# Where the two halves of an attention output are added: on VectorE and GpSimd, or by an accumulating load

## The chip, the cores and the metric

The kernel runs on one core of a Trainium2 chip. Its time is the device time of one execution in microseconds; the figure to predict is the median of several executions. Names of the engines as the profile writes them: PE is TensorE's matrix multiplication, PEld its loading of weights, DVE is VectorE, ACT is ScalarE, POOL is GpSimd, and SP is SyncE, which here does nothing but issue transfers (DMAs). ACT and POOL can issue transfers too.

## The reference

One step of a hybrid encoder with two layers, of width 1024, on 1024 prompt tokens and on 8 streams of 16 sample tokens. Layer A has sliding-window attention with its own K and V, layer B has chunked attention over K and V that are shared; each is followed by a squared-ReLU MLP with 4096 hidden units.

```python
def attend(q, k, v, bias, sink):
    s = jnp.einsum('bqhgd,bkhd->bhgqk', qg, k) * (HEAD_DIM ** -0.5)   # 16 heads, 4 KV heads, d = 64
    s = s + bias                                   # A: ALiBi, 2 chunks back; B: relative bias, 8 chunks back
    p = softmax(s)                                 # A: with a learned sink per head
    o = jnp.einsum('bhgqk,bkhd->bqhgd', p, v)
    return o.reshape(b, tq, N_HEADS * HEAD_DIM)

for layer in range(2):
    hp = hp + attend(...) @ w_o[layer]
    hp = hp + square(relu(rmsnorm(hp, g_mlp[layer]) @ w_up[layer])) @ w_down[layer]
```

## The kernel before

Tokens are in nine tiles of 128: tiles 0 to 7 are the prompt, tile 8 (`ST`) the sample. All matrix products are of float32 numbers that are split into a high part, rounded to `float32r`, and the low rest. `split` does this with a copy on ScalarE (or GpSimd) and a subtraction on VectorE. A product then takes three matmuls: high by high, high by low, low by high.

Each layer runs through four stages: attention, the output projection (`wo_phase`), the MLP's first product (`mlp_up`) and its second (`mlp_down`). The change is in the first two.

**Attention.** The prompt's work is cut into 32 groups `(t, j)`, a query tile and a KV head with its four query heads, in two passes: heads 0 and 1 for all tiles, then heads 2 and 3. For a group, `score_a` or `score_b` makes the scores on PE, the row minimum on DVE, the exponential on ACT and the normalisation of the probabilities `p` on POOL (lines L403 in A, L481 and L526 in B). Scores run two or three steps ahead of their use. `V(g)` then transposes `p` on PE (L324), splits it, and multiplies it with V (`pv_mm`, L331 and L332). V's high and low parts lie side by side in the columns of one operand, so the result `ps_pv` has 128 rows: rows 0 to 63 are the product with the high part of V and rows 64 to 127 that with the low part. **The two halves must be added**, and that is where the change is. Between a group's matmuls the kernel weaves those of other work, among it the projections of the next tiles and, late in the stage, the output projections `WO(t, half)`.

In layer A (`o2=0`), `pv_out` copies the lower half from PSUM on ACT (L357) and adds the halves on DVE with two additions (L359) into a tile `oT`; after the second group of a tile one store sends it to DRAM (`oTd`, L1540). In layer B (`o2=1`), `pv_store` copies all 128 rows on ACT (L346) and stores both halves apart in `oTd` with four transfers of 64 KB from SP (L351).

**Output projection.** `WO` inside the attention stage and `load_o` in `wo_phase` fetch the attention's output of a tile by `load_halves`, split it and multiply it with the output weights. In A that is one load of 256 KB (L337). In B a second load brings the other half (L339), and an addition joins them: on POOL inside the attention stage, and on DVE in `wo_phase` (both L341). In B the high part of the split inside the attention stage is made on POOL too (L130).

The order of instructions on every engine is fixed when the program is built: a scheduler places them by an estimate of when each can start. At run time an engine takes its instructions in that order, and one that waits holds up all behind it. On SP and POOL this holds for transfers as well: an issue waits until what it needs is there.

Of the kernel before, what the change touches and what calls it, by code (L numbers as in the profile page):

```python
# [8 lines left out]
F32 = mybir.dt.float32  # L9
F32R = mybir.dt.float32r  # L10
AF = mybir.ActivationFunctionType
ALU = mybir.AluOpType
# [4 lines left out]
P = 128  # L17
D = 1024
KC = D // P
NT = 8  # L20
# [74 lines left out]
class Build:  # L95
# [238 lines left out]
    def load_halves(self, layer, half, t, a, b, e=None):  # L334
        nc = self.nc
        src = self.oTd[layer][half][t]
        nc.sync.dma_start(a, src[:, 0])  # L337
        if self.o2[layer] and t < NT:
            nc.sync.dma_start(b(), src[:, 1])  # L339
            e = e or (nc.gpsimd if self.o2[layer] == 1 else nc.vector)  # L340
            e.tensor_tensor(a, a, self.last, ALU.add)  # L341
# [10 lines left out]

    def pv_out(self, apool, pv, oT, j):
        nc = self.nc
        t = apool.tile([64, 2, 2, P], F32, tag="pvt", name="pvt", bufs=1)
        pv4 = pv.rearrange("p (a b q) -> p a b q", a=2, b=2)
        nc.scalar.copy(t, pv4[64:128])  # L357
        for par in range(2):
            nc.vector.tensor_tensor(  # L359
                oT[par * 64 : par * 64 + 64, 2 * (j % 2) : 2 * (j % 2) + 2, :],  # L360
                pv4[0:64, :, par, :],
                t[:, :, par, :],
                ALU.add,
            )
# [278 lines left out]
    def wo_phase(self, layer, sx, x8, wo):  # L643
        nc = self.nc
        with ExitStack() as st:
            self.psum_pools(st, f"wo{layer}", dict(m=(4, 1), g=(3, 1)), dict(m="m", n="g"))
            work = self.pool(st, f"wow{layer}")
# [18 lines left out]
            def load_o(t, z):  # L666
# [3 lines left out]
                self.last = oh.bitcast(F32)  # L670
                self.load_halves(layer, 1, t, o, lambda: self.last, nc.vector)
# [586 lines left out]
    def run(self):  # L1258
# [9 lines left out]
        with ExitStack() as top:  # L1268
# [21 lines left out]
            def dram(shape, name):  # L1290
                return dp.tile(shape, F32, tag=name, name=name)
# [3 lines left out]
                    [dram([P, 2 if t < NT and CFG[l]["o2"] else 1, 4, P], f"oTd{l}_{b}_{t}")  # L1295
# [10 lines left out]
            self.o2 = [c["o2"] for c in CFG]  # L1306
# [57 lines left out]
    def attention(self, layer):  # L1364
# [18 lines left out]
        with ExitStack() as st:  # L1383
# [25 lines left out]
            hts, qTs, qss, kss, probs, oTs, xr = {}, {}, {}, {}, {}, {}, {}  # L1409
# [121 lines left out]
            def O(g, pv):  # L1531
                t, j = groups[g]
                if self.o2[layer]:
                    self.pv_store(apool, pv, self.oTd[layer][j // 2][t], j)
                    return
                if j % 2 == 0:
                    oTs[t] = work.tile([P, 4, P], F32, tag="oT", name="oT")
                self.pv_out(apool, pv, oTs[t], j)
                if j % 2 == 1:
                    nc.sync.dma_start(self.oTd[layer][j // 2][t][:, 0], oTs[t])  # L1540
# [35 lines left out]
            def addend():  # L1576
                self.last = self.scratch([P, 4, P], F32, "o2")
                return self.last

            def WO(t, half):  # L1580
                o = self.scratch([P, 4, P], F32, "o")
                self.load_halves(layer, half, t, o, addend)
# [243 lines left out]
def make_plan(tail, second):  # L1826
    plan = {}
    for s in range(2 * NT):
# [29 lines left out]
        la=3, prio=0, xt={('A', 8): 'x', ('B', 7): 'x', ('B', 0): 'keep', ('B', 4): 'keep'}, late=0, eng='cgu', k2=3, q2=9, lead=3, sf=0, up=(99, 2, 0, 3), ld=((9, 9, 10, 10), (11, 11, 12, 13), (26, 27, 28, 29)), n='g', q='g', qrb=1, np=3, bias_bufs=3, p_bufs=3, psp=(), wr='mmmm', wt=(0, 0, 2, 0, 2, 2, 0, 0, 2), rx=1, kd=1, o2=0, sb=0),  # L1858
    dict(banks=dict(g=(4, 1), s=(3, 1), m=(1, 1)), q_bufs=4, order={}, second=SECOND[1], plan=make_plan({15: [('A', 0)], 17: [('A', 1)], 19: [('A', 2)], 21: [('A', 3)], 23: [('A', 4)], 25: [('A', 5)], 27: [('A', 8)], 28: [('A', 7)], 29: [('A', 6)], 31: [('B', 0), ('B', 4), ('B', 1)], 32: [('B', 5), ('B', 2), ('B', 3)]}, SECOND[1]),
        la=2, prio=1000, xt={('B', 0): 'keep', ('B', 4): 'keep', ('B', 1): 'hh', ('B', 5): 'hl', ('B', 2): 'hh', ('B', 3): 'hl'}, late=0, eng='Ogu', k2=3, q2=6, lead=9, sf=0, up=(4, 2, 0, 99), ld=((11, 11, 11, 11), (11, 11, 11, 11), (26, 27, 28, 29)), n='g', q='g', qrb=2, np=2, bias_bufs=2, p_bufs=10, psp=(), wr='mmmm', wt=(0, 0, 0, 1, 1, 1, 1, 1, 2), rx=0, kd=1, o2=1, sb=3),  # L1860
# [45 lines left out]
```

## Time and profile before

| | |
|---|---|
| median of 3 runs | 2360.16 us (2359.15 to 2361.63) |
| the profiled execution's own time | 2354.01 us |
| its span, first to last instruction | 2352.2 us |
| mean granted clock of TensorE | 0.997 |
| PE busy | 2271.4 us, 97% of the span |
| DVE busy | 1715.4 us, 73% |
| ACT busy | 1332.4 us, 57% |
| POOL busy | 635.3 us, 27% |
| DMA | 392.70 MB, mean 167 GB/s |

Attention A runs from the start to about 380 us, the projections behind it to about 445, and the MLP of layer A to about 1140. Attention B lasts to about 1620, its last projections to about 1663, and the MLP of layer B to the end. In rows of groups, the count stands behind `x`, then come the busy time in us, the mean of one in ns, and the idle time of the engine just before, with what ended it. The issue of a transfer by SP is not counted as busy time of any engine.

### The profile page before, as it was taken

Reading aid. Unit: us, or ns where it says so; the run is one execution under the profiler, and the core shown is the slowest. Engines: PE = TensorE matmul, PEld = TensorE weight load, DVE = VectorE, ACT = ScalarE, POOL = GpSimd, SP = SyncE. Lnnn points to the kernel's source line nnn. Section 1 sums busy time; section 2 is a strip of 40 time slices with the busy share of each in tenths; the row PEclk is TensorE's granted clock in tenths of the full one; section 3 lists DMA queues with packets and bytes.
Section 4 is the critical chain, followed back from the end, with each engine's and each line's share of the span. In section 5 each row is a group of like instructions: output and inputs, shape, how many; then the busy total and the mean of one; then the engine's idle time right before and its main releaser. Section 6 shows DMA issues by size and latency. Waiting matters only on the chain.

```text
span 2352.2 us, 33396 instructions
## 1 busy us (share of the span) xinstructions
PE 2271.4 (97%) x11429; PEld 1893.3 (80%) x11429; DVE 1715.4 (73%) x3075; ACT 1332.4 (57%) x2684; POOL 635.3 (27%) x950
## 2 busy tenths in 40 slices
PE   7998999899999999999999999998899999999999
PEld 6787887788888888777877788887788888888787
DVE  6788786766656578899577877777666566678987
ACT  3777674655555555344377666665655555565443
POOL 4334332313213111002333434344132132110011
PEclk9999999999999999999999999999999999999999
DMA  7335546234434677748653655555244343977567
GB/s 253 127 113 163 171 147 202 95 122 160 137 111 151 218 230 177 267 147 214 183 157 113 193 157 177 174 168 184 69 156 138 113 162 107 284 209 199 175 169 192
DMA packets 226715, 392.70 MB, mean 167 GB/s; under 512 B 51592, under 2 KB 126288, under 8 KB 226448
## 3 DMA queue, kind: packets, MB, share of 16 engines
q1 hardware_dynamic: 188816, 283.58, 37.4%
q0 software_dynamic: 36432, 102.26, 15.9%
q10 hardware_dynamic: 1296, 4.72, 0.5%
q8 instruction: 90, 1.47, 0.2%
q14 instruction: 81, 0.66, 0.1%
HBM read 236.51 MB, written 156.85 MB: 167 GB/s over the span
## 4 chain that ended last, share of the span: by engine, by line
PE 74%; DVE 9%; DMA 9%; ACT 3%; issue 3%; POOL 1%; SPq 0%; ACTq 0%; DVEq 0%; POOLq 0%
PE ps_c L743 6%; PE ps_c L744 6%; PE ps_c L745 6%; PE ps_x L743 5%; PE ps_x L745 5%; PE ps_x L744 5%; PE ps_mm L217 3%; PE ps_mm L219 3%; PE ps_mm L218 3%; PE ps_y L745 2%; PE ps_y L743 2%; PE ps_y L744 2%; PE ps_tr L324 2%; DMA a<-hd 2%; DVE w L134 1%
## 5 line engine op out<-in xcount | busy, mean ns | idle before, releaser
L744 PE MATMUL ps_c<-w,a 128*128 128x512 f32 x960 | 374.7, 390 | 6.9 <-DVE w L134 6.9
L743 PE MATMUL ps_c<-w,a 128*128 128x512 f32 x960 | 375.1, 391 | 5.1 <-DVE x L1174 3.1
L745 PE MATMUL ps_c<-w,a 128*128 128x512 f32 x960 | 374.3, 390 | 0.0
L908 POOL DMA_DIRECT2D hd<-h x272 | 148.9, 550 | 594.8 <-ACT h L817 378.2
L743 PEld LDWEIGHTS ps_c<-w,a 128*128 128x128 f32 x960 | 180.6, 188 | 46.3 <-issue 4.7
L744 PEld LDWEIGHTS ps_c<-w,a 128*128 128x128 f32 x960 | 180.7, 188 | 46.1 <-DVE w L134 9.0
L745 PEld LDWEIGHTS ps_c<-w,a 128*128 128x128 f32 x960 | 180.5, 188 | 37.5
L128 ACT CAST a<-a 128x1536 fp32r<-128x1536 f32 x80 | 118.6, 1482 | 149.5 <-DMA a<-hd 149.5
L217 PE MATMUL ps_mm<-w,hh 128*128 128x512 f32 x432 | 172.7, 401 | 8.8 <-POOL w L185 3.3
L134 DVE TENSOR_TENSOR a<-a 128x1536 fp32r<-128x1536 f32 x80 | 140.5, 1756 | 45.7 <-ACT a L128 45.7
L219 PE MATMUL ps_mm<-w,hl 128*128 128x512 f32 x432 | 171.7, 398 | 1.5 <-DMA hl<-hTd 1.4
L218 PE MATMUL ps_mm<-w,hh 128*128 128x512 f32 x432 | 170.8, 396 | 1.3 <-DVE w L190 1.1
L743 PE MATMUL ps_x<-sx,w 128*128 128x512 f32 (+1 forms) x408 | 157.8, 387 | 3.7 <-ACT h L864 2.7
L128 ACT CAST w<-s 128x2048 fp32r<-128x2048 f32 x56 | 107.1, 1912 | 92.2 <-DVE s L1060 80.7
L128 ACT CAST w<-ru 128x512 fp32r<-128x512 f32 (+1 forms) x160 | 110.0, 708 | 83.9 <-PE ps_y L744 32.0
L745 PE MATMUL ps_x<-sx,w 128*128 128x512 f32 (+1 forms) x408 | 154.1, 378 | 0.0
L744 PE MATMUL ps_x<-sx,w 128*128 128x512 f32 (+1 forms) x408 | 154.1, 378 | 0.0
L134 DVE TENSOR_TENSOR w<-s,w 128x2048 fp32r<-128x2048 f32 x56 | 128.1, 2288 | 32.4 <-ACT w L128 32.3
L1179 POOL DMA_DIRECT2D xp<-o x28 | 36.3, 1296 | 411.8 <-ACT o L1162 390.2
L134 DVE TENSOR_TENSOR ptl<-ps_tr,pth 128x512 fp32r<-128x512 f32 x180 | 122.4, 685 | 24.1 <-ACT pth L128 18.2
L134 DVE TENSOR_TENSOR w<-ru,w 128x512 fp32r<-128x512 f32 (+1 forms) x160 | 126.6, 793 | 14.7 <-ACT w L128 14.6
L816 ACT ACTIVATE h<-h 128x512 f32<-128x512 f32 (+1 forms) x102 | 61.9, 607 | 122.6 <-DVE h L866 93.5
(274 smaller groups left out, 6131.4 us busy)
## 6 DMA issues: line engine op xcount, KB each, us to landing
a<-hd SPq DMA_DIRECT2D x80, 768.0 KB, 6.2
hd<-h POOLq DMA_DIRECT2D x272, 192.0 KB, 2.5
ru<-in_w_up SPq DMA_DIRECT2D x64, 512.0 KB, 3.9
r<-in_w_down SPq DMA_DIRECT2D x32, 1024.0 KB, 10.0
xp<-o POOLq DMA_DIRECT2D x28, 768.0 KB, 9.4
o<-oTd SPq DMA_DIRECT2D x50, 256.0 KB, 5.0
x<-xp SPq DMA_DIRECT2D x23, 512.0 KB, 5.2
xp<-xo SPq DMA_DIRECT2D x18, 512.0 KB, 2.8
```

Of the source, the lines that this page charges most:

```text
L128: a = nc.scalar.copy(hi, src)
L134: return a, e.tensor_tensor(lo, src, hi.bitcast(F32), ALU.subtract)
L217: nc.tensor.matmul(ps, a, w[:, 0, k, :], start=(k == 0), stop=False)
L218: nc.tensor.matmul(ps, a, w[:, 1, k, :], start=False, stop=False)
L219: self.lp = nc.tensor.matmul(ps, b, w[:, 0, k, :], start=False, stop=(k == KC - 1))
L324: self.lp = nc.tensor.transpose(pt[:, i, :], get(i), self.ident)
L743: a = mm(ps, ah, bh, start=first, stop=False, skip_group_check=True)
L744: mm(ps, ah, bl, start=False, stop=False, skip_group_check=True)
L745: return a, mm(ps, al, bh, start=False, stop=last, skip_group_check=True)
L816: a = nc.scalar.activation(t, src, AF.Relu)
L908: return lambda p, z: self.nc.gpsimd.dma_start(self.hd[c // 4][:, p, c % 4], z)
L1179: nc.gpsimd.dma_start(dst, z, accum_op=ALU.add)
```

## The change

Both layers now store the two halves apart with `pv_store`. `load_halves` loads the first half on SP as before, and then issues from POOL a second transfer that adds the other half to it on its way (`accum_op`), once the first has landed. `pv_out`, the tile `oT`, the second load's tile and the additions on DVE and POOL are gone.

```diff
-    def load_halves(self, layer, half, t, a, b, e=None):
+    def load_halves(self, layer, half, t, a):
         nc = self.nc
         src = self.oTd[layer][half][t]
         nc.sync.dma_start(a, src[:, 0])
-        if self.o2[layer] and t < NT:
-            nc.sync.dma_start(b(), src[:, 1])
-            e = e or (nc.gpsimd if self.o2[layer] == 1 else nc.vector)
-            e.tensor_tensor(a, a, self.last, ALU.add)
+        if t < NT:
+            nc.gpsimd.dma_start(a, src[:, 1], accum_op=ALU.add)
...
-    def pv_out(self, apool, pv, oT, j):
-        nc = self.nc
-        t = apool.tile([64, 2, 2, P], F32, tag="pvt", name="pvt", bufs=1)
-        pv4 = pv.rearrange("p (a b q) -> p a b q", a=2, b=2)
-        nc.scalar.copy(t, pv4[64:128])
-        for par in range(2):
-            nc.vector.tensor_tensor(
-                oT[par * 64 : par * 64 + 64, 2 * (j % 2) : 2 * (j % 2) + 2, :],
-                pv4[0:64, :, par, :],
-                t[:, :, par, :],
-                ALU.add,
-            )
...
-                self.last = oh.bitcast(F32)
-                self.load_halves(layer, 1, t, o, lambda: self.last, nc.vector)
+                self.load_halves(layer, 1, t, o)
                 self.split(oh, ol, o)
...
             def O(g, pv):
                 t, j = groups[g]
-                if self.o2[layer]:
-                    self.pv_store(apool, pv, self.oTd[layer][j // 2][t], j)
-                    return
-                if j % 2 == 0:
-                    oTs[t] = work.tile([P, 4, P], F32, tag="oT", name="oT")
-                self.pv_out(apool, pv, oTs[t], j)
-                if j % 2 == 1:
-                    nc.sync.dma_start(self.oTd[layer][j // 2][t][:, 0], oTs[t])
+                self.pv_store(apool, pv, self.oTd[layer][j // 2][t], j)
...
             def WO(t, half):
                 o = self.scratch([P, 4, P], F32, "o")
-                self.load_halves(layer, half, t, o, addend)
+                self.load_halves(layer, half, t, o)
```

By the built programs, PE has the same instructions in both, in an order that differs in places of the two attention stages and of `wo_phase`. DVE loses 64 additions in A and 2 in B, POOL loses 14 additions in B and gains 32 accumulating loads, 16 in each layer. SP gains 128 stores in A and loses 16 there, and loses 16 loads in B. Three places show how the order moves; lines below the changed functions have lower numbers in the changed kernel (L403 becomes L388, L481 becomes L466, L1540 is gone).

On SP in attention A, around the store of tile 1's first output (`oTd_0_1`; KT is the transposed K, whose halves are copied across by two transfers, `qu` and `kb` belong to the sample's units), the rows before:

```order
L545 DMA qu<-qT8d_0_125 128x128
L546 DMA qu<-qT8d_0_125 64x128
L547 DMA qu<-qT8d_0_125 64x128
L549 DMA kb<-kT8d_133 128x32
L313 DMA KT<-KT 64x4x128
L314 DMA KT<-KT 64x4x128
L1540 DMA oTd_0_1_76<-oT 128x512
L1421 DMA x<-in_x_prompt 128x1024
```

and the same place in the changed program:

```order
L349 DMA oTd_0_1_76<-pvt 64x2x128 x4
L530 DMA qu<-qT8d_0_125 128x128
L531 DMA qu<-qT8d_0_125 64x128
L532 DMA qu<-qT8d_0_125 64x128
L534 DMA kb<-kT8d_133 128x32
L313 DMA KT<-KT 64x4x128
L349 DMA oTd_0_1_76<-pvt 64x2x128
L314 DMA KT<-KT 64x4x128
L349 DMA oTd_0_1_76<-pvt 64x2x128 x3
L1404 DMA x<-in_x_prompt 128x1024
```

Eight small stores take the place of one large one, four of them ahead of the unit's loads and one between the two copies of KT.

On POOL in attention A, around the first output projection (`qrs` is a norm of the queries, `kc` and `uks` belong to the sample's units, `p` is the normalisation), the rows before:

```order
L238 TENSOR_TENSOR qrs<-qms,mhalf 128x8
L403 TENSOR_SCALAR p<-p,li 128x256 x4
L568 COPY uks<-kc 128x2x64
L403 TENSOR_SCALAR p<-p,li 128x256 x4
L569 TENSOR_TENSOR uks<-kc,uks 128x2x64
L558 TENSOR_TENSOR kc<-kc,gq 128x128
```

and in the changed program:

```order
L238 TENSOR_TENSOR qrs<-qms,mhalf 128x8
L339 DMA o<-oTd_0_0_75 128x512
L388 TENSOR_SCALAR p<-p,li 128x256 x4
L553 COPY uks<-kc 128x2x64
L554 TENSOR_TENSOR uks<-kc,uks 128x2x64
L388 TENSOR_SCALAR p<-p,li 128x256 x4
```

The accumulating load of tile 0 now stands ahead of a group's normalisations of `p`.

On POOL near the end of attention B (`xp` is the store of a projected tile, `mrs` a norm), the rows before:

```order
L1616 DMA xp_112<-xo 128x1024
L341 TENSOR_TENSOR o<-o,o_16937 128x512
L130 COPY oh<-o 128x512
L481 TENSOR_SCALAR p<-p,li 128x640 x2
L568 COPY uks<-kc 128x2x64
L341 TENSOR_TENSOR o<-o,o_16948 128x512
L569 TENSOR_TENSOR uks<-kc,uks 128x2x64
L130 COPY oh<-o 128x512
```

and in the changed program:

```order
L1588 DMA xp_112<-xo 128x1024
L339 DMA o<-oTd_1_5_107 128x512
L339 DMA o<-oTd_1_2_104 128x512
L130 COPY oh<-o 128x512
L466 TENSOR_SCALAR p<-p,li 128x640 x2
L553 COPY uks<-kc 128x2x64
L554 TENSOR_TENSOR uks<-kc,uks 128x2x64
L339 DMA o<-oTd_1_3_105 128x512
L130 COPY oh<-o 128x512
```

The additions are replaced by accumulating loads, and the cast `oh` stands right behind the issue whose landing it needs.

More of the change, by code (lines that the diff above doesn't have):

```diff
@@ L1294, in run @@
                 [
-                    [dram([P, 2 if t < NT and CFG[l]["o2"] else 1, 4, P], f"oTd{l}_{b}_{t}")
+                    [dram([P, 2 if t < NT else 1, 4, P], f"oTd{l}_{b}_{t}")
                      for t in range(NTILE)]
@@ L1305, in run @@
             self.qT8d = [[dram([P, 512], f"qT8d{l}_{j}") for j in range(KV)] for l in range(2)]
-            self.o2 = [c["o2"] for c in CFG]
             self.kT8d = [dram([P, KV, P], f"kT8d{l}") for l in range(2)]
@@ L1408, in attention @@
             second = cfg["second"]
-            hts, qTs, qss, kss, probs, oTs, xr = {}, {}, {}, {}, {}, {}, {}
+            hts, qTs, qss, kss, probs, xr = {}, {}, {}, {}, {}, {}
             x_src = self.x_in if A else lambda t: self.xd[t]
@@ L1574, in U @@
                 return self.unit(up, small, layer, bp, j, v8, gq8, ck, cv)
-            def addend():
-                self.last = self.scratch([P, 4, P], F32, "o2")
-                return self.last
             def WO(t, half):
                 o = self.scratch([P, 4, P], F32, "o")
-                self.load_halves(layer, half, t, o, addend)
+                self.load_halves(layer, half, t, o)
                 kind = cfg["wt"][t] if half else 0
```

4 lines of the change are left out of this document (2 added, 2 removed).

## The prediction

> **What bounds the kernel now.** I read the page first: busy shares and the shares of the chain that ended last.
>
> ```profile
> PE 2271.4 (97%) x11429; PEld 1893.3 (80%) x11429; DVE 1715.4 (73%) x3075; ACT 1332.4 (57%) x2684; POOL 635.3 (27%) x950
> PE 74%; DVE 9%; DMA 9%; ACT 3%; issue 3%; POOL 1%; SPq 0%; ACTq 0%; DVEq 0%; POOLq 0%
> ```
>
> TensorE (PE) is busy for 97% of the span, and the change takes no matmul away. So only time in which PE stands idle can be won, and only new idle time can be lost. The next view cuts the four stretches that the change touches: attention A, the projection phase behind it, attention B with its projections, and the end of B.
>
> ```profile
> core 0: us, PE busy (x) PEld busy (x) DVE busy (x) ACT busy (x) POOL busy (x), PEclk, DMA share, GB/s
> 60.00:380.00 320.00, 304.94 (x1677) 251.74 (x1676) 257.88 (x832) 230.34 (x670) 118.27 (x214) 0.99 0.49 152
> 380.00:450.00 70.00, 63.71 (x359) 52.70 (x358) 52.13 (x77) 34.99 (x64) 28.52 (x26) 1.00 0.40 136
> 1140.00:1590.00 450.00, 432.30 (x2363) 359.09 (x2362) 338.47 (x941) 291.54 (x806) 188.13 (x257) 1.00 0.54 167
> 1590.00:1670.00 80.00, 67.03 (x387) 55.07 (x386) 60.66 (x96) 44.07 (x91) 32.48 (x29) 0.96 0.43 145
> ```
>
> PE idles 320 - 304.94 = 15.1 us in attention A, 6.3 behind it, 17.7 in attention B and 13.0 at its end. That is 52 us in all, and the first 15 are where most of the removed work stood. What ended them is in the list of PE's waits between 60 and 380 us (waited for, total, times, longest):
>
> ```profile
> PE ps_mm L176 <- DVE xo L1614: 2.3, 3, 1.5
> PE ps_s L380 <- ACT p L395: 2.2, 4, 0.9
> PE ps_pv L331 <- ACT pth L128: 2.1, 1, 2.1
> PE ps_tr L324 <- POOL p L403: 1.7, 2, 0.9
> PE ps_s L380 <- DMA KT<-KT: 1.2, 2, 0.9
> ```
>
> No wait is large and no engine owns them. PE follows a fixed order with short slack to all the others.
>
> **The change part by part.** First, VectorE (DVE) in attention A. The rows of the removed additions and of the output copies, before and as layer B already does them:
>
> ```profile
> L359 DVE TENSOR_TENSOR oT<-ps_pv,pvt 64x256 f32<-64x256 f32 x64 | 26.6, 415 | 3.4 <-ACT pvt L357 2.8
> L357 ACT COPY pvt<-ps_pv 64x512 f32<-64x512 f32 x32 | 18.7, 583 | 3.6 <-PE ps_pv L332 3.0
> L346 ACT COPY pvt<-ps_pv 128x512 f32<-128x512 f32 x32 | 19.1, 597 | 5.1 <-PE ps_pv L332 4.8
> ```
>
> 64 additions of 415 ns are 26.6 us, a tenth of DVE's 257.9 us in that stretch. ScalarE's copy goes from 583 to 597 ns, 32 x 14 ns = 0.4 us, which its idle time hides (230 of 320 busy). DVE is 81% busy there, so it is not the bound; it is late now and then. Of the quoted waits, those for xo, ScalarE's p and POOL's p go through DVE, directly or because DVE feeds the engine named: 2.3 + 2.2 + 1.7 = 6.2 us. With a tenth of DVE's work gone a third of them may go: I take -2.0 us, with 0 and -7 (half of the stretch's 15.1) as ends.
>
> Second, SyncE (SP), which issues the stores and is used in order. By what it issues for the output tensor (count, then min/median/max in ns):
>
> ```profile
> L351 SPq DMA_DIRECT2D oTd<-pvt x128: 574/605/1462, 1202.4 to 1614.9; - x128
> L1540 SPq DMA_DIRECT2D oTd<-oT x16: 319/326/383, 87.3 to 377.2; - x16
> L339 SPq DMA_DIRECT2D o<-oTd x14: 319/332/537, 1348.4 to 1578.6; - x14
> ```
>
> Attention A gets 128 stores of 605 ns, 77.4 us, in place of 16 of 326 ns, 5.2 us: 72 us more of SP's time in 320. In B SP loses 16 loads of 0.33 us, 5.3 us. Queued behind the new stores are the KT copies, the units' loads and the loads of hh, hl and xo. In the changed order a KT copy has a 605 ns store between its two halves at the place shown above, and the stores of one group delay what follows by 4 x 0.605 = 2.4 us. PE waited for KT only twice in 320 us. I take +1.5 us; nothing shown excludes 0, and eight KT pairs at 0.6 us end it at +5.
>
> Third, GpSimd (POOL) in attention A, which gets eight accumulating loads before the last groups and eight around the end. None of this size into SBUF is in the trace. The nearest rows are 256 KB accumulations into DRAM (the issue's own time, then time to landing), and layer B's additions, which wait on POOL for the same loads:
>
> ```profile
> L1165 POOL DMA_DIRECT2D xp<-x x9: 850/860/1257, 1119.0 to 2338.4; - x9
> DMA to landing us min/median/max: 3.7/4.8/6.5
> POOL o L341 <- DMA o<-oTd: 29.4, 12, 6.9
> L341 POOL TENSOR_TENSOR o<-o,o 128x512 f32<-128x512 f32 x14 | 18.0, 1286 | 33.9 <-DMA o<-oTd 29.4 <-DVE li L478 4.4
> L908 POOL DMA_DIRECT2D hd<-h x272: 539/539/1135, 464.2 to 2062.7; - x136
> ```
>
> An accumulation must wait until the plain load has landed, and POOL stands in that wait: 29.4 / 12 = 2.4 us each in B. With 0.86 us for the issue a POOL stop is 3.3 us. Behind it on POOL stand the normalisations of p, for which PE's transposes wait. Their cover is read from two timelines, POOL's and PE's:
>
> ```profile
> 307.92 1.84 POOL L403 TENSOR_SCALAR p<-p,li 128x256 f32<-128x256 f32 x4 [5.94 <-DVE li L416]
> 326.35 1.84 POOL L403 TENSOR_SCALAR p<-p,li 128x256 f32<-128x256 f32 x4 [5.73 <-DVE li L416]
> 341.19 1.84 POOL L403 TENSOR_SCALAR p<-p,li 128x256 f32<-128x256 f32 x4 [3.37 <-DVE nm L390]
> 314.62 0.66 PE L324 MATMUL ps_tr<-identr,p 128*128 128x128 f32 x4
> 330.57 1.09 PE L324 MATMUL ps_tr<-identr,p 128*128 128x128 f32 x8
> 341.73 1.34 PE L324 MATMUL ps_tr<-identr,p 128*128 128x128 f32 x6 [0.89 <-POOL p L403]
> ```
>
> The first two groups are ready at 309.76 and 328.19, 4.9 and 2.4 us before their transposes; the third is already late by 0.9. POOL is idle for 3 to 6 us before each, so a stop of 3.3 us mostly fits in. Ten such places (eight loads, and two at the end) at 0.25 us exposed give +2.5; fully covered it is 0, and eight at 1 us, less cover than the third group shows, are +8.
>
> [...]
>
> Fourth, the projections behind attention A. From SP's timeline, the loads between 360 and 372 us, and the projection that uses them:
>
> ```profile
> 363.61 0.93 SPq L337 DMA_DIRECT2D o<-oTd  x2
> DMA to landing us min/median/max: 3.1/6.0/6.8
> L176 PE MATMUL ps_wo<-w,oh x72: 387/389/496, 386.0 to 1634.1; 128*128 128x512 f32 x72
> ```
>
> The two loads land near 370, and PE takes them up from 386 on: 16 us for an accumulation of 4.8. The landing is covered; what is left is POOL's issue between the sums that PE's transposes need, so +0.5 (ends -1 and +3).
>
> Fifth, layer B. POOL loses 14 additions of 1.286 us, 18.0, and gains 16 issues of 0.86, 13.8. It keeps its first wait, and where its cast of oh stands right behind the accumulation it gets a second one for the landing, up to 4.8 us. POOL is idle for 450 - 188 = 262 us, which takes most of it: +1.5, with -2 (the work it loses) and +5 (one uncovered landing) as ends.
>
> Sixth, the end of B: SP's first load with the landings of that moment, the chain of waits (start, length), and the timelines of DVE and PE:
>
> ```profile
> 1592.87 0.38 SPq L337 DMA_DIRECT2D o<-oTd  x1
> DMA to landing us min/median/max: 2.1/2.5/2.8
> 1592.01 2.10 DMA oTd<-pvt
> 1594.18 3.97 DMA oh<-oTd
> 1598.18 0.69 DVE o L341
> 1598.87 0.60 DVE xo L1614
> 1598.18 0.69 DVE L341 TENSOR_TENSOR o<-o,oh 128x512 f32<-128x512 f32 x1 [2.05 <-DMA oh<-oTd]
> 1599.62 0.47 PE L176 MATMUL ps_mm<-w,oh 128*128 128x512 f32 x1 [1.01 <-DVE l L477]
> ```
>
> Two things change. The accumulation must wait for the first load, 1592.87 + 2.5 to 2.8, so it is issued near 1595.7 and by the 4.8 us row lands near 1600.5, where the sum stood at 1598.9: 1.6 us later. But DVE no longer stops for 2.05 us with xo behind it, and it was that stop which cost PE 1.0 us. I take +1.0, with -2 and +4. [...]
>
> **The sum.** -2.0 + 1.5 + 2.5 + 0.5 + 1.5 + 1.0 = +5.0 us. The profiled execution took 2354.01 us, its span 2352.2 and 1.8 around it, and comes to 2359.0. It lies 6.15 below the median of the timed runs, 2360.16; I let that difference stand, so the forecast is 2365.
>
> **The rivals.** *VectorE's relief decides.* PE in attention A moves with the latest of many short waits, and each of 32 groups has 0.83 us less on DVE ahead of its next minimum and split. If half of PE's 15 us goes with it (-7), the accumulations sit inside POOL's idle time and B's end gains its 1 us, the time is about 2352. It decides as soon as a POOL stop stays below the 3 to 6 us of idle time before each p. For it: DVE feeds ScalarE and POOL there. Against it: DVE is 81% busy, and of the quoted waits only the one for xo names it.
>
> *SP becomes late.* With 72 us more in 320 and each store waiting for ScalarE's copy, loads of hh, hl and xo come late. If half of the 32 store groups delay PE by 1 us, less DVE's 2, that is +14, 2374. Against it: B lives with the same stores, and its PE idles 17.7 of 450 us, no more than A's 15.1 of 320.
>
> *Nothing moves.* Gains and stops cancel, or all stay under cover: 2360. That the additions stay is no rival: the new program's order has 32 accumulating loads and none of them.
>
> **How the numbers follow.** A measurement of this kernel tells 0.2%, 4.7 us, from no change. The forecast's case, slower by 5 (own range -1 to +12, 2359 to 2372), gets 0.42: 0.30 of it beyond 0.2% and 0.12 within. SP late gets 0.13, nothing moves 0.13, VectorE's relief 0.32. So faster 0.32, same 0.25, slower 0.43. The range of 2349 to 2377 reaches past the faster rival's time and the late SP's, and leaves out about a tenth on each side.
>
> **What would show it.** Right: DVE's busy time between 60 and 380 us down by about 26; POOL waiting for o<-oTd about 2 us each, now on the accumulating line, in A too; PE's waits for p up by 2 to 3 us; accumulations landing 4 to 5 us after issue. Wrong: PE's idle time in attention A falling below 10 us (VectorE's relief), or rising by over 10 with waits for hh, hl, xo or KT (SP), or accumulations that land in 2 to 3 us, which would make B's end a gain.

## The result, and the profile after

| | before | after |
|---|---|---|
| median | 2360.89 us (4 runs, 2359.15 to 2363.2) | 2378.25 us (4 runs, 2373.66 to 2383.3) |
| ratio to before | | 1.0074, 95% interval 1.0058 to 1.009 |
| profiled execution, span | 2354.01, 2352.2 us | 2373.66, 2371.9 us |

The change makes the kernel slower by 17 us. The prediction said slower by 5, with a range up to 2377. The changed kernel was measured once more with the experiments: 1.0064 (1.0048 to 1.0081), 15 us. Microseconds "over before" below are a ratio's excess times 2360.

First the page of after, its busy times:

```profile
PE 2284.3 (96%) x11429; PEld 1899.9 (80%) x11429; DVE 1693.9 (71%) x3009; ACT 1325.5 (56%) x2684; POOL 644.8 (27%) x968
```

The matmuls are the same 11429, but PE is busy for 12.9 us longer (2271.4 before). So matmuls took longer, and the span and the mean granted clock (TensorE's, as a share of full speed) say why. Before:

```profile
core 0: 2352.2 us, clock 0.997
```

And after:

```profile
core 0: 2371.9 us, clock 0.992
```

0.3% of 2352 us is 7 us lost to the clock, 0.8% of 2372 is 19: 12 us more, close to PE's 12.9. The span's other 6.8 us are idle time. This is one pair of executions; over many, the clock's share is smaller, as the last experiment shows. Two of the four stretches shown of before, attention A and B (us, then busy time of each engine, clock, DMA):

```profile
60.00:380.00 320.00, 301.15 (x1646) 247.26 (x1645) 229.58 (x756) 219.43 (x658) 128.62 (x225) 0.98 0.59 164
...
1140.00:1590.00 450.00, 428.79 (x2300) 352.96 (x2299) 325.22 (x896) 281.64 (x768) 176.03 (x245) 0.99 0.56 162
```

VectorE's busy time in the window of attention A falls by 28.3 us, near the 26 that were said. A part of that is work that the slower kernel does behind 380 us (PE has 31 matmuls fewer in the window); over the whole span VectorE is relieved of 21.5 us. Still PE idles 18.9 us in A's window in place of 15.1; in B's it is 21.2 in place of 17.7. PE's waits between 60 and 380 us:

```profile
PE ps_mm L176 <- DVE xo L1586: 5.8, 3, 4.5
PE ps_tr L324 <- POOL p L388: 3.3, 2, 2.9
PE ps_pv L331 <- ACT pth L128: 2.7, 2, 2.1
```

The wait for KT has fallen from 1.2 to 0.5 us, and a single one of 4.5 us, for xo, stands at the head of the list. The accumulating loads (issue on POOL, then who waited for them, then the time to landing):

```profile
L339 POOL DMA_DIRECT2D o<-oTd x32: 857/915/1239, 201.5 to 1639.9; - x32
...
  DMA o<-oTd: 11.0, 7
...
  ACT oh L128: 24.5, 10
  POOL oh L130: 6.3, 2
...
DMA to landing us min/median/max: 3.9/4.4/7.8
```

The landing is 4.4 us where 4.8 was assumed, but 7.8 at worst. POOL stands 11.0 us before its issues; ScalarE, which the prediction did not name, stands 24.5 us in front of its cast of oh. Near the end of attention A the casts of three tile halves follow each other. The timelines of ACT, DVE and PE there, and the clock behind it:

```profile
376.87 0.62 ACT L128 CAST oh<-o 128x512 fp32r<-128x512 f32 x1 [6.39 <-DMA o<-oTd]
...
377.51 0.69 DVE L134 TENSOR_TENSOR ol<-o,oh 128x512 fp32r<-128x512 f32 x1 [7.87 <-ACT oh L128]
378.12 0.68 DVE L1586 TENSOR_TENSOR xo<-ps_mm,xo 128x512 f32<-128x512 f32 x1
...
378.86 0.80 PE L176 MATMUL ps_mm<-w,oh 128*128 128x512 f32 x1 [4.51 <-DVE xo L1586]
379.46 0.63 PE L177 MATMUL ps_mm<-w,oh 128*128 128x512 f32 x1
...
378.00:384.00 6.00, 5.14 (x12) 4.08 (x13) 2.60 (x5) 2.31 (x5) 0.86 (x1) 0.50 1.05 264
```

ACT stands with the cast for 6.4 us, DVE behind it with the low half ol for 7.9, and behind ol, in DVE's fixed order, stands the addition xo of the tile half before, whose product had long been there. PE needs the PSUM bank that xo reads, and stops for 4.5 us. After the stop the granted clock is 0.50: a matmul takes 0.63 us in place of 0.39 for the next five microseconds. At A's first accumulation, the timelines of POOL, PE and ACT:

```profile
201.48 1.14 POOL L339 DMA_DIRECT2D o<-oTd  x1 [4.17 <-DVE nm L375]
202.33 2.16 POOL L388 TENSOR_SCALAR p<-p,li 128x256 f32<-128x256 f32 x4
...
203.22 0.48 PE L324 MATMUL ps_tr<-identr,p 128*128 128x128 f32 x1 [2.87 <-POOL p L388]
...
207.23 0.62 ACT L128 CAST oh<-o 128x512 fp32r<-128x512 f32 x1 [1.79 <-DMA o<-oTd]
...
209.33 0.50 PE L331 MATMUL ps_pv<-pth,VS 128*128 128x512 f32 x1 [2.12 <-ACT pth L128]
```

The issue stands in front of p (PE's stop was 0.8 us at this place before, now 2.9), and the cast stands in front of pth. In attention B it is POOL that casts, and the same happens (POOL, then PE):

```profile
1556.61 1.16 POOL L130 CAST oh<-o 128x512 fp32r<-128x512 f32 x2 [3.73 <-DMA o<-oTd]
...
1557.83 0.55 PE L176 MATMUL ps_mm<-w,oh 128*128 128x512 f32 x1 [1.82 <-POOL oh L130]
```

### The profile page after: what moved, and what is told of

The parts are those of the page before. It is cut to its first block, busy times and chain, and to the rows that moved or that the text cites. A ratio compares the mean times of both kernels' runs of the same rounds, so it can differ in the third digit from the quotient of the medians.

```text
span 2371.9 us, 33506 instructions
## 1 busy us (share of the span) xinstructions
PE 2284.3 (96%) x11429; PEld 1899.9 (80%) x11429; DVE 1693.9 (71%) x3009; ACT 1325.5 (56%) x2684; POOL 644.8 (27%) x968
## 4 chain that ended last, share of the span: by engine, by line
PE 70%; DMA 11%; DVE 8%; ACT 4%; issue 3%; POOL 1%; SPq 1%; ACTq 0%; DVEq 0%; POOLq 0%
PE ps_c L728 7%; PE ps_c L727 7%; PE ps_c L729 7%; PE ps_x L727 5%; PE ps_x L729 5%; PE ps_x L728 5%; PE ps_mm L217 3%; DMA a<-hd 3%; PE ps_mm L218 3%; PE ps_mm L219 3%; PE ps_y L729 2%; PE ps_y L727 2%; PE ps_y L728 2%; PE ps_tr L324 2%; PE ps_mm L176 1%
## 5 line engine op out<-in xcount | busy, mean ns | idle before, releaser
L128 ACT CAST w<-s 128x2048 fp32r<-128x2048 f32 x56 | 107.1, 1912 | 91.1 <-DVE s L1044 79.5
L128 ACT CAST pth<-ps_tr 128x512 fp32r<-128x512 f32 x180 | 105.2, 594 | 47.7 <-PE ps_tr L324 43.0
```

The lines of the kernel that those rows point to most:

```text
L128: a = nc.scalar.copy(hi, src)
```

## The experiments

Three theories stood against each other. **Waits**: an engine that stands with a cast behind the landing holds up what PE needs. **Stores**: SP's 128 new stores, or VectorE's changed place, are the cost. **Clock**: each longer stop of PE is followed by matmuls at half speed, so it is paid twice. All results in one table:

| run | ratio to before (95%) | us over before |
|---|---|---|
| accumulating load in A only | 1.0042 (1.0026 to 1.0058) | 9.9 |
| accumulating load in B only | 1.0038 (1.0024 to 1.0053) | 9.0 |
| A: stores, two plain loads, addition on GpSimd | 1.0061 (1.0044 to 1.0078) | 14.4 |
| A: the same, addition on VectorE | 1.005 (1.0033 to 1.0067) | 11.8 |
| both: second load plain, nothing added | 1.0026 (1.0014 to 1.0038) | 6.1 |
| loads a group ahead of the casts | 1.0048 (1.003 to 1.0066) | 11.3 |
| six tile halves of A as before | 1.0101 (1.0077 to 1.0126) | 23.8 |
| A only: second load plain, nothing added | 1.0013 (1.0001 to 1.0026) | 3.1 |
| B only: second load plain, nothing added | 1.0006 (0.9993 to 1.0019) | 1.4 |
| xo ahead of ol at A's end | 1.0074 (1.0058 to 1.0089) | 17.5 |
| half of each second load accumulated | 1.0071 (1.0056 to 1.0087) | 16.8 |
| after, once more | 1.0064 (1.0048 to 1.0081) | 15.1 |

**One layer at a time.** `load_halves` keeps the way of before and gets the accumulating load for one layer:

```diff
+            if self.o2[layer] == 3:
+                nc.gpsimd.dma_start(a, src[:, 1], accum_op=ALU.add)
+                return
             nc.sync.dma_start(b(), src[:, 1])
```

> Only attention A stores its halves and adds them by the accumulating load; layer B as before. The sum of the prediction gives its four terms in A, +2.5 us. The theory of the waits (ScalarE and GpSimd stand in program order behind the landing of the accumulating load, and TensorE waits for probabilities and h behind them) gives attention A's +8 us of after and two or three more behind it, +9 to +12 us in all, about half of it as idle time of TensorE. The theory of the granted clock (each idle stretch of TensorE of about 2 us or more is followed by 3.4 us or more at half speed) expects no other total but another split: busy time of TensorE up by 4 to 7 us with the same matmuls, and 10 to 14 us more of half speed than before in attention A and right behind it. If A costs under 4 us, the loss of after lies in B.

> Only attention B adds by the accumulating load (it stored its halves before, too); attention A as before. The sum of the prediction gives its two terms in B, +2.5 us. The theory of the waits gives attention B's +6.7 us of after, less what the output projection and the MLP's end give back, +5 to +8 us. The theory of the granted clock: of that half as busy time of TensorE, from 5 to 10 us more at half speed. If it costs under 1 us, the loss in after's B comes from A's state at B's start and not from B's own accumulating loads.

Each layer costs 9 to 10 us, and together they make after's 15 to 17. The sum of the prediction had 2.5 for each. In the run with B alone, the place shown above is worse (POOL, PE, then the clock from 1548 to 1557 us):

```profile
1549.12 2.18 POOL L130 CAST oh<-o 128x512 fp32r<-128x512 f32 x2 [5.65 <-DMA o<-oTd]
...
1551.35 0.79 PE L176 MATMUL ps_mm<-w,oh 128*128 128x512 f32 x1 [4.68 <-POOL oh L130]
...
1548.00:1557.00 9.00, 5.65 (x19) 4.58 (x19) 3.34 (x9) 3.17 (x9) 6.65 (x9) 0.62 0.67 234
```

**A without an accumulating load.** A is given B's way of before, with the addition on GpSimd (`o2=1`) or on VectorE (`o2=2`):

```diff
-    dict(banks=dict(g=(5, 1), ..., kd=1, o2=0, sb=0),
+    dict(banks=dict(g=(5, 1), ..., kd=1, o2=1, sb=0),
```

> Attention A stores its halves like after, but loads both by SP and adds them on GpSimd, as layer B of the kernel before does; no accumulating load anywhere. This holds A's stores and VectorE's relief (28 us less work) against the accumulating load. If the stores by SP are the cost (rival that SP becomes late): +5 us or more, with waits for KT, h or x. If the accumulating load's issue and landing are the cost: within 3 us of before, either way, since GpSimd's additions have about a microsecond each and wait for plain loads. The theory of the granted clock expects half-speed time within 5 us of before in the second case.

> As the run before, with the additions of attention A's halves on VectorE in place of GpSimd: VectorE is relieved of some 28 us in A and gets 16 additions back. If the stores are the cost: like the run with GpSimd's additions, +5 us or more. If the accumulating load is the cost: within 3 us of before; if GpSimd's place in front of the probabilities is what counts and not the landing, this one is faster than the run with GpSimd's additions by 2 us or more, since nothing of the change is left on GpSimd in A.

Both came out at 14.4 and 11.8, which by their expectations speaks for the stores. But they also move other things. PE's waits for p in A go from 1.7 to 5.0 us with GpSimd's additions and to 6.6 with VectorE's. In the 30 us from the MLP's first matmul of `ps_x` on, PE idles 10.4 and 7.7 us, where it idled 4.9 before (6.4 in after).

So these two don't tell the stores from the additions. The next ones do.

**The addition left out.** The second load is plain and overwrites the first, in both layers or in one:

```diff
-            nc.gpsimd.dma_start(a, src[:, 1], accum_op=ALU.add)
+            nc.gpsimd.dma_start(a, src[:, 1])
```

> As after, but GpSimd's second load is a plain one that overwrites the first: the addition is left out, the queue, the size and the order of the two loads stay. If the accumulation itself is what makes the second load slow, its landing falls from 4.4 us to the 2 to 3 us of a plain transfer, ScalarE's and GpSimd's casts wait correspondingly less, and the time falls by 6 to 12 us. If a second load behind a first is the cost, whatever it does on landing, the landing stays near 4 us and the time within 4 us of after's 2378.

> Only attention A stores its halves, and its second load is a plain one: the addition is left out; layer B as before. It divides A's cost (10 us with the accumulating load) into what the accumulation does and what the stores, the second load and VectorE's relief do together. If the landing of the accumulation (4.4 against 3.2 us, up to 7.8 near A's end) carries it, this is within 4 us of before, with no stop of TensorE over 2 us near 380 us; if the stores carry it, it stays at 7 us or more.

> Only attention B, second load plain and the addition left out; attention A as before. It divides B's cost (9 us with the accumulating load) in the same way. The run with both plain took 6 us more than before, so the two runs of this kind should add up to 6 us. Theory of the landing: 1 to 5 us here, as GpSimd still stands behind a landing of 3 us in place of its own addition. If B costs 7 us or more here, it is the wait of GpSimd and ScalarE for any second load and not the accumulation that makes B slow.

With both plain, the order of instructions is the same as after's on every engine, and 9 to 11 of the 15 to 17 us are gone. Each layer's plain run has the order of its run with the accumulating load, too. The accumulation alone costs 9.9 - 3.1 = 6.8 us in A and 9.0 - 1.4 = 7.6 in B, each uncertain by some 5 us. All else (stores, relief of VectorE, the second load behind the first) is 3.1 us in A and within the measurement's noise in B: the theory of the stores falls as the main cause. An addition on an engine was no cheaper in A: over the plain loads it cost 11.3 us on GpSimd and 8.7 on VectorE, though in another order of instructions. The plain second loads (issue on POOL, landing):

```profile
L339 POOL DMA_DIRECT2D o<-oTd x32: 536/596/788, 199.6 to 1632.7; - x32
...
DMA to landing us min/median/max: 2.9/3.6/7.7
```

The issue is 0.32 us shorter and the median landing 0.8. That seems little for 10 us. What it does is seen at A's end. ACT's wait with the cast and PE's wait for xo between 345 and 400 us, in the plain run:

```profile
ACT oh L128 <- DMA o<-oTd: 6.5, 4, 2.6
...
PE ps_mm L176 <- DVE xo L1586: 1.9, 3, 0.9
```

In after:

```profile
ACT oh L128 <- DMA o<-oTd: 7.2, 2, 6.4
...
PE ps_mm L176 <- DVE xo L1586: 5.8, 3, 4.5
```

Three of these loads overlap there. The plain ones land 3.7, 5.3 and 5.5 us after their issue, the first of them 4 us ahead of the others, and the casts get through between them. The accumulating ones, issued in the same order, take 7.5, 6.7 and 7.7 us. The longest wait goes from 2.6 to 6.4, PE's stop from 0.9 to 4.5, and behind 0.9 the clock stays at 1.00:

```profile
378.00:384.00 6.00, 5.58 (x28) 3.98 (x26) 2.40 (x5) 2.45 (x8) 0.43 (x1) 1.00 1.00 338
```

**Half of the accumulation.** Only the first half of each tile half is accumulated, the rest of the addition is left out:

```diff
-            nc.gpsimd.dma_start(a, src[:, 1], accum_op=ALU.add)
+            nc.gpsimd.dma_start(a[:, 0:2], src[:, 1, 0:2], accum_op=ALU.add)
```

> As after, with the accumulating load reading only half of each tile half (128 KB in place of 256): half of the addition is left out. Its landing should fall to 3 to 3.5 us while GpSimd's issue stays at 0.8 to 0.9 us (the number of partitions is the same). If the landing carries the accumulation's 11 us, the time falls to the run with both loads plain, 5 to 9 us over before; if the issue on GpSimd carries it, it stays at 14 to 18 us over before. A few instructions of the projections change places, which can move either by some 3 us.

Issue and landing of the 128 KB:

```profile
L339 POOL DMA_DIRECT2D o<-oTd x32: 858/917/1238, 202.2 to 1640.3; - x32
...
DMA to landing us min/median/max: 3.0/3.5/7.2
```

The issue is as long as with 256 KB, the landing as short as the plain one, and the time stays: 16.8. By its expectation that speaks for the issue on GpSimd. At A's end, though, the wait for the landing rules. ACT's and PE's longest waits there in this run, and in the second run of after:

```profile
ACT oh L128 <- DMA o<-oTd: 4.8, 2, 4.4
...
PE ps_mm L176 <- DVE xo L1586: 5.3, 5, 2.5
```

```profile
ACT oh L128 <- DMA o<-oTd: 8.5, 2, 7.7
...
PE ps_mm L176 <- DVE xo L1586: 7.4, 3, 5.8
```

Over four runs ACT's longest wait is 2.6, 4.4, 6.4 and 7.7 us and PE's stop 0.9, 2.5, 4.5 and 5.8: the stop is the wait less 1.7 to 1.9. So at this one place ScalarE's wait for the landing sets the stop. The sum of such waits doesn't set the time: over the whole program ScalarE stands in front of the cast for 4.2 us before, 19.7 with both loads plain (6.1 us over before), 13.3 here (16.8 over before), and 24.5 and 28.0 in the two profiles of after. Since some instructions of the projections changed places in this run, how the whole 10 us divide into landing and issue stays open.

**Loads ahead of the casts.** Both loads of a tile half are written one group earlier, into buffers of their own (in layer B every second one keeps the old buffer), but for at most two tile halves of a group; the other loads of the last groups stay where they were:

```diff
+                for c, t in plan.get(g + 1, ())[:2]:
+                    if c in "AB":
+                        early["AB".index(c), t] = LO(t, "AB".index(c))
...
-                o = self.scratch([P, 4, P], F32, "o")
-                self.load_halves(layer, half, t, o)
+                o = early.pop((half, t), None) or LO(t, half)
```

> As after, with both loads of a tile half written one group (about 10 us) before the casts that read it, into buffers of their own, so that casts on ScalarE and GpSimd don't stand behind the landing. Theory of the waits: the waits of the casts for o<-oTd (24.5 us on ScalarE, 6.3 on GpSimd in after) all but vanish, TensorE's stop of 4.5 us near the end of attention A and the one of 1.8 us in B go, and with them the half-speed stretches right behind them (6.8 us each); 8 to 14 us faster than after, about 2366. If the stores by SP or GpSimd's issue time are the cost, this stays within 3 us of after.

Four to six us better than after, less than the 8 to 14 expected, and the intervals overlap. ACT's waits with the cast (whole program, 24.5 us before this edit):

```profile
ACT oh L128 <- DMA o<-oTd: 12.8, 3, 6.8
...
PE ps_uo L598 <- ACT pts L594: 3.4, 2, 3.2
```

They halve, and the stop at xo is gone (1.5 us in all), but a stop of 3.2 us for pts is new. On GpSimd the waits grew: 8.3 us in front of its casts (6.3 before this edit) and 21.1 in front of its issues (11.0). At A's end ScalarE still stands 5.6 us for a landing there. The direction is that of the theory of the waits, but the size is not, and the run doesn't prove it.

**Two places as before.** `pv_out` comes back for six tile halves of A, those of the first and the last projections:

```diff
+        return t < NT and (layer or (half, t) not in ((0, 0), (0, 6), (0, 7), (1, 0), (1, 4), (1, 7)))
```

> As after, but in attention A the six tile halves of the first and of the last projections (the ones at the two places where TensorE stopped for 2.9 and 4.5 us) are added on VectorE as in the kernel before; the other ten of A and all of B keep the accumulating load. If A's 10 us hang on those two places: 5 to 9 us faster than after, near the 2369 of the run with B alone, though 80 of the 128 stores stay. If the stores or the ten other accumulations carry the cost: within 3 us of after, or 3 to 4 us for the six sixteenths left out.

A miss: 6 to 9 us slower than after. The stops moved. PE's waits between 60 and 400 us:

```profile
PE ps_mm L176 <- DVE xo L1609: 6.4, 4, 2.9
PE ps_s L381 <- DMA xo<-in_x_sample: 2.7, 1, 2.7
```

Four shorter stops for xo replace the long one, and one for a transfer of SP's is new. Taking the load off two places didn't mend it; the edit moved other instructions as well, and which of them made the new stops is not shown.

**xo ahead of ol.** The narrowest edit: at A's end DVE takes xo first, so that it doesn't stand with ol. Some instructions of ACT and DVE between 234 and 260 us changed places, too.

```diff
+                    if A and done:
+                        self.behind(done[-1], r[1])
```

> After, with the accumulating loads kept, and near the end of attention A the low half ol of a tile half placed on VectorE behind the first addition of xo of the tile half before it, where after has it in front; only some ten instructions change places, all near 370 to 385 us, and nothing in B. TensorE's stop of 4.5 us for xo there was said to come from VectorE standing with ol behind the landing. By that theory the stop falls below 2 us and the half-speed stretch of 6.8 us behind it goes: 4 to 8 us less than after. If the stop comes from the store or from the loads themselves, it stays, as a wait of TensorE for oh or ol, and the time is after's within 3 us.

Another miss: the time is after's. PE's stop for xo has indeed shrunk to 0.9 us. PE's timeline now, and ACT's:

```profile
380.03 0.53 PE L565 MATMUL ps_us<-kb,qu 128*128 128x288 f32 x2 [1.89 <-ACT kb L561]
...
382.69 0.80 PE L176 MATMUL ps_mm<-w,oh 128*128 128x512 f32 x1 [0.94 <-DVE xo L1596]
383.28 0.63 PE L177 MATMUL ps_mm<-w,oh 128*128 128x512 f32 x1
...
378.16 0.62 ACT L128 CAST oh<-o 128x512 fp32r<-128x512 f32 x1 [6.65 <-DMA o<-oTd]
```

Twelve matmuls came earlier, but ACT still stands with the cast for 6.65 us, with kb and pth behind it, and PE stops for kb and a little later for xo: 1.9 and 0.9 us within 4.6. The clock fell all the same (0.63 us for a matmul again). The wait only changed its name: at this place ACT's wait for the landing is the cause, and DVE's was one of its ways to PE.

**The clock by itself.** Two kernels leave the whole computation out and run a stream of 128x512 matmuls with stops of set lengths, while VectorE works. In short:

```python
ps = burst(110 + 7 * rep)                               # matmuls, weights g
nc.vector.tensor_tensor(b[:, 0:64], ps[:, 0:64], b[:, 0:64], ALU.min)
nc.vector.tensor_tensor(b[:, 0:m], b[:, 0:m], b[:, 0:m], ALU.min)   # m = 0 to 4096
nc.vector.tensor_tensor(g, s[:, 0:128], b[:, 0:128], ALU.max)       # the next burst waits for g
```

> Not the kernel's computation: 7840 matmuls of 128x512 on one core in 60 bursts of 25 to 32 us (the first of them longer), and between two bursts TensorE waits for VectorE, which works through 0 to 4096 elements in a row, so for some 0.5 to 5 us; each length comes five times. It measures the granted clock alone. If an idle stretch of TensorE takes the clock down, the half-speed stretches (3.4 or 6.8 us) follow the gaps above a length near 2 us, nearly always above 3 us, never below 1.5, and start at the gap's end or up to 3.4 us around it. If they come from something else in the kernel (DMA traffic, power of all engines together), none or few are seen here, and they don't depend on the gap.

Three bursts of 117 matmuls (start, length, and the stop ahead of it in brackets):

```profile
551.77 26.77 PE L49 MATMUL burst<-a,g 128*128 128x512 f32 x117 [1.73 <-DVE g L54]
580.53 28.38 PE L49 MATMUL burst<-a,g 128*128 128x512 f32 x117 [2.00 <-DVE g L54]
611.18 28.38 PE L49 MATMUL burst<-a,g 128*128 128x512 f32 x117 [2.26 <-DVE g L54]
```

A stop of 1.73 us costs itself; the ones of 2.00 and 2.26 cost 1.6 us more, half of a stretch of 3.4 us at half speed. Over the 59 stops, half speed followed none of the 20 up to 1.73 us, 8 of 20 from 2.0 to 2.8, 8 of 10 of 3.1 and 3.6, and all 9 of 4.1 and 5.2. It began 2.3 to 5.0 us after the stop's beginning and lasted 3.4 or 6.8 us. This is one execution, with a mean granted clock of 0.972. No engine but VectorE was at work beside TensorE during these stops: in eight windows of 6 to 10 us around some of them ACT and POOL were busy for 0.00 us, and the share of the DMA engines was 0.00.

> Not the kernel's computation: a stream of 128x512 matmuls on one core, with four kinds of stops, ten of each: one of 3.06 us; two of 1.46 us with 4 matmuls (0.9 us) between them; two of 1.46 us with 12 matmuls (2.8 us) between them; two of 1.46 us far apart. If the granted clock follows the length of one stop, only the first kind is followed by half-speed stretches, in 8 of 10. If it follows the share of idle time in some window of 3 to 4 us, the second kind is hit too, nearly as often as the first, the third sometimes and the fourth never.

The bursts of 110 behind the first three kinds, in one round (start, length, the stop just ahead):

```profile
127.12 26.80 PE L49 MATMUL burst<-a,g 128*128 128x512 f32 x110 [3.06 <-DVE g L55]
...
158.54 26.63 PE L49 MATMUL burst<-a,g 128*128 128x512 f32 x110 [1.73 <-DVE g L55]
...
191.60 25.18 PE L49 MATMUL burst<-a,g 128*128 128x512 f32 x110 [1.73 <-DVE g L55]
```

The stops meant to be 1.46 us were 1.73. After one stop of 3.06, and after two of 1.73 with 1.2 us of matmuls between, 110 matmuls took 26.8 and 26.6 us; after two with 3.0 us between, 25.2. The counts are 8 of 10, 7 of 10, none of 10, and none for stops far apart. So stops that stand close together add up: two of 1.73 us within 4.6 us did, seven times in ten, and within 6.4 us they did not. In the run with xo first, 1.9 and 0.9 us within 4.6 fit this.

The clock's own records bear on why equal stops fared differently. In each stream all half-speed stretches (25 and 15) begin on one fixed grid with a step of 3.413 us, and so do the 4 in before's profile and the 10 in after's. Cut by its grid into slices, before's profile behind its first 16 us has four full-speed slices with 2.22 to 2.76 us of PE idle, each followed by half speed, and none of the others, with 1.78 us or less, was followed by it (in the first 16 us slices with up to 3.12 us were not). Of the three stops quoted from the first stream, those of 2.00 and 2.26 us lie whole in one slice, and of the 1.73 us some 1.5 do. The author's reading is that a stop of 2.0 to 2.8 us was paid twice when enough of it fell into one slice, which is chance. In after's profile the border is less sharp: slices with 1.63 and 1.82 us of idle time were followed by half speed, one with 1.65 was not.

**After once more.**

> The changed kernel once more, unaltered. If its first runs were typical: 1.006 to 1.009 times before, attention B between 431 and 441 us, and in attention A again a stop of 4 us or more near 379 us with a half-speed stretch behind it. If attention B's extra time is chance (which stops fall into the clock's window), its half-speed time differs from the first profile's 6.8 us by 3.4 us or more while its idle time is nearly the same.

The stop at A's end was 5.8 us, with a half-speed stretch of 6.8 behind it again. Attention B, from its first transposition of p to its first `ps_wo`, took 431.3 us against 431.2 in the first profile, with 3.4 us at half speed in place of 6.8, so the time hung less on it there than expected. In the three other profiles with B in the same order it took 434.4, 440.1 and 441.0 us, with 6.8 to 20.5 us at half speed.

**Where the time is, over many executions.** One pair of profiles doesn't settle the clock's share: before's 0.997 is higher than that of any of its 54 later timed runs (mean 0.9934; after's ten: 0.9918). Span times one less the clock is the time lost to it: 15.6 us before and 19.5 after on the mean, so 3.9 of the 16.1 us by which these spans differ, give or take some 1 us. Idle time is the span less PE's busy time: 80.8 us in before's profile and 79.5 to 82.6 in the three with plain loads, but 87.6 and 88.2 in the two of after (86.9 and 89.2 with one layer alone). So of the 16 us some 7 are idle time, some 4 the clock, and some 5 the record doesn't divide.

The runs with one layer changed give more profiles of the same order (one of A with xo moved). Mean of attention with the projections behind it, per layer, from the first transposition of p to the MLP's first `ps_x`:

| | profiles | length | PE idle | half of the half-speed time |
|---|---|---|---|---|
| A as before | 3 | 362.5 us | 15.6 | 3.4 |
| A as after | 4 | 371.7 | 19.2 | 7.7 |
| B as before | 5 | 454.3 | 21.0 | 1.9 |
| B as after | 5 | 463.9 | 24.9 | 7.5 |

By these profiles each layer loses 9 to 10 us: 3.5 in A and 3.9 in B as idle time, 4.3 and 5.6 in half speed; at most 1.4 is in neither. But two of the five of B as after (six tile halves of A as before, xo ahead of ol) come from the slowest execution of their kernel, at a clock of 0.986 and 0.985. Without them B loses 5.5 us, 2.1 of them idle and 2.7 in half speed. So half speed is a quarter of the loss by the timed runs and half of it by these profiles; its exact share stays open.

## Why the prediction was wrong

**The step that failed** is the price of the accumulating loads. The sum had +2.5 for them in A and +2.5 for layer B; one layer alone costs 9.9 and 9.0 us, and 6.8 and 7.6 of that go when the second load is plain. A sentence of its first part failed with it: "only time in which PE stands idle can be won, and only new idle time can be lost". By it a stop costs its own length. Idle time did rise by only some 7 us, not far from the sum's 5.0. But PE was also busy longer with the same matmuls, by 12.9 us in the first pair of profiles, and the clock makes some 4 of the 16 us over the timed runs. The page of before had shown it: the clock stood at 0.96 in the stretch from 1590 to 1670 us, where the kernel before has stops of 2.0 and 2.4 us close together. The stream of matmuls shows it by itself: two microseconds of idle time can cost 3.6. There a stop of 2.0 us was followed by half speed three times in five, and two of 1.73 close together seven times in ten.

**VectorE's relief (-2.0).** Its work fell much as said. What that brought can't be told from the terms beside it: A with plain second loads is 3.1 us over before.

**SP's stores (+1.5).** With the accumulation left out, stores, relief and the chain of two loads together make 3.1 us (0.2 to 6.1), and KT isn't among PE's longer waits. The rival that SP becomes late had +14; it fell as the main cause.

**The accumulating loads in A (+2.5, 0 to +8).** This is the term that was mis-sized: the accumulation alone is 6.8 us. POOL in front of p was rightly named (1.7 us of PE's waits before, 3.3 after) and is the smaller part. By PE's waits the larger way goes through ACT, whose cast of oh stands behind the landing, with pth and DVE's ol and xo behind it (xo: 2.3 us before, 5.8 after). The prediction followed POOL's queue and not that of the engine that reads the loaded tile.

**The projections behind A (+0.5).** The cover of 16 us was read at PE, up to the first matmul of `wo_phase`. But ScalarE reads the tile first, and before the change it already stood for the first of the two loads that the prediction quotes, issued at 363.61 us:

```profile
367.22 0.62 ACT L128 CAST oh<-o 128x512 fp32r<-128x512 f32 x1 [2.73 <-DMA o<-oTd]
```

So there was no cover on ScalarE, and the landing there was 6.7 to 7.7 us after the change (8.3 to 9.3 in the second profile), not 4.8.

**Layer B (+1.5 and +1.0).** Measured 9.0. The mechanism named, POOL's cast behind the accumulation, is the right one: 3.7 and 5.7 us of waiting where up to 4.8 was allowed for one place. What was missing is again the half speed behind it (2.8 of 8.2 us in the timed runs with B alone), and that such places come more than once.

**The rivals.** *VectorE's relief decides* fell: its point was POOL's stops staying inside POOL's idle time, but at A's first accumulation PE stood 2.9 us for p, and at A's end it was ACT's stop that reached PE. *Nothing moves* fell. Accumulations that land in 2 to 3 us, which would have made B's end a gain, were not seen either: the landing was 4.4 us (3.9 at least), and 3.6 (2.9 at least) for the plain load of the same size. GpSimd's issues took 0.86 to 1.24 us each, close to the 0.85 to 1.26 in the row of before.

## What to carry to other kernels

When a load replaces an addition, ask who reads the loaded tile first, and what stands behind that reader on its engine: the landing can be paid there and on every engine down the line, and moving one instruction moved the wait to the next here. On a kernel with its matrix engine 97% busy, reckon with what the stream of matmuls showed: a stop of 2 us or more, or two of 1.7 within 4.6 us, can cost up to nearly twice its length (2.00 us cost 3.6; half speed followed two in five of the single stops from 2.0 to 2.8 us and seven in ten of the pairs), and look at the granted clock by stretches for where that already happens. Try the cheapest bound first: with the addition simply left out both layers still were 6 us slower than before, so with these stores and loads in this order no faster way of adding could have made the change a gain.

## What the runs showed of the hardware

- An accumulating load from DRAM into SBUF, 256 KB issued by GpSimd: issue 0.92 us, landing 4.4 us; plain, in the same order of instructions, 0.60 and 3.6. With 128 KB the issue stays at 0.92 and the landing is 3.5.
- Of transfers that overlap near the end of attention A, three accumulating ones landed 6.7 to 7.7 us after their issue (8.3 to 9.3 in a second execution), three plain ones after 3.7, 5.3 and 5.5.
- In the stream of matmuls TensorE's granted clock fell to one half for 3.4 or 6.8 us after a stop of 2.0 us in three of five cases, after 4.1 us in all, and after none of 20 single stops of 1.73 us or less. The stretches begin on a grid of 3.413 us. In before's profile, behind its first 16 us, half speed followed the four slices of that grid with 2.22 us of idle time or more and none of the full-speed ones with 1.78 or less; in after's it followed one with 1.63 and not one with 1.65.
